# The first product of a feed-forward block in a two-layer decoder trunk: seven products instead of eight for three of eight row pairs

## The chip, the core and the metric

The kernel runs on one core of a Trainium2 chip, as one launch. The metric is device time in microseconds (us). Three runs of the kernel before gave 2171.43, 2171.99 and 2173.27 us; the median is 2171.99.

The engines are named as in the profile: PE (the matrix engine; PEld are its weight loads), DVE (vector), ACT (scalar), POOL, and SP, whose queue issues most DMAs. Every engine, and every queue, works through its instructions in the order in which they stand.

## The reference

256 tokens (T) of width 2048 (D) pass two layers. Each layer is a norm, a token mixer and a residual addition, then a norm, a SwiGLU feed-forward and a residual addition. The first mixer is a chunkwise mLSTM, the second a gated linear recurrence. All is float32. The part that changes is the feed-forward:

```python
D_FF = ((8 * D_MODEL // 3 + 255) // 256) * 256      # 5632

def swiglu(x, w_in, w_out):
    g, u = jnp.split(x @ w_in, 2, axis=-1)
    return (jax.nn.silu(g) * u) @ w_out

h = h + swiglu(rms_norm(h, norm_ffn[layer]), ffn_w_in[layer], ffn_w_out[layer])
```

x @ w_in is the first product (2048 rows of weights, 2 x 5632 columns), the one with w_out the second.

## The kernel before

**Precision.** A float32 product is made of three products in the type fp32r: every operand is split into hi (a cast, on ACT) and lo (operand minus hi, on DVE), and hi*hi, hi*lo and lo*hi are summed in one of eight PSUM banks. For weights, `halves` (L153) makes whi on ACT (L156) and wlo on DVE (L158) from the loaded tile raw; for features, `split_store` (L316) does it (L318, L319).

**Streaming.** `stream` (L165) goes through a weight matrix two rows of 128 (k, k + 1) and 512 columns at a time. Such a load is 512 KB on SP's queue (L77). The tiles raw, whi and wlo have four buffers each, so the fifth remainder wlo waits until PE has used up the first, and a load waits for the remainder made from its buffer. A scheduler orders the instructions of each engine when the program is built; weight preparation has a raised priority there.

**Two forms of product.** `linear_tok` (L179) has tokens on PSUM's partitions: the features are the stationary operand, the weights move, 512 columns a matmul (L187, L188, L189), six matmuls a row k for two blocks of 128 tokens. `linear_wide` (L208) has output features on the partitions: whi is stationary and hi and lo of the features (2 x 256 tokens) move together (L214), then wlo with hi (L217); eight matmuls a row k, four of 512 and four of 256 columns. `gather` (L223) then adds the two halves.

**The feed-forward** (`ffn`, L548) loops over eleven groups of 512 inner features. For each it makes g and u with `linear_wide` over 16 rows, gathers them, multiplies them by the norm's factor per token (a row spread over the partitions, `bc`), applies SiLU, multiplies, and splits the result into hh and hl (L319). After all eleven, `project_out` (L303) makes the second product with `linear_tok`: four output quarters (po) over 44 rows of inner features, each added to the residual h by DVE (L312).

**The norms.** `Norm.quarter` (L249) transposes a quarter of h (eight transposes, tr), scales it and splits it; it is queued in `pending` and run between two rows of the product that follows (`run_pending`, L148). `finish` (L288) makes the factor per token, and with `bcast` spreads it with a matmul (bc).

Of the kernel before, what the change touches and what calls it, by code (L numbers as in the profile page):

```python
# [27 lines left out]
AHEAD = 1000  # L28

# [4 lines left out]
def kernel(  # L34
# [111 lines left out]
    pending = []  # L146

    def run_pending():  # L148
        if pending:
            pending.pop(0)()  # L150
# [28 lines left out]
    def linear_tok(w, c0, nk, act, name, ncols=NB, lag=0):  # L179
# [12 lines left out]
        for k, hi, lo in stream(w, c0, nk, ncols):  # L192
# [4 lines left out]
            if k > 1:  # L197
                run_pending()
# [9 lines left out]
    def linear_wide(w, c0, nk, act, act2, name, soon=2):  # L208

        ps = [acc(f"{name}_{f}") for f in range(4)]  # L210
        for k, hi, lo in stream(w, c0, nk):
# [7 lines left out]
            if k >= soon:  # L219
                run_pending()  # L220
# [81 lines left out]

    def project_out(w, nk, act, nxt):  # L303

        for q in range(4):
            ps = linear_tok(w, q * NB, nk, act, f"po{q}", lag=nxt.lag if q == 3 else 0)
            for b in range(NT):
                if q == 3 and nxt.lag:
# [4 lines left out]
            if q < 3 or not nxt.lag:  # L313
                pending.append(lambda q=q: nxt.done(q))
# [34 lines left out]
    for q in range(1, 4):  # L349
        pending += [lambda q=q: n0.quarter(q), lambda: None]  # L350
    n1 = Norm("f0", par["g_ffn"][:, 0:16], bcast=True)

    def mlstm_mixer():
        with tc.tile_pool(name="mx", bufs=2) as mx:
            w = m_w_in[0]
            ys = [[mx.tile([P, 4, T], F32R, tag=f"y{s}{j}", name=f"y{s}{j}", bufs=1) for s in "hl"] for j in range(4)]
            sel = mx.tile([H, H, P], F32R, name="sel", bufs=1)
# [72 lines left out]
            pending.append(gate_rows)  # L430


            qT = mx.tile([P, H, T], F32, name="qT", bufs=1)
# [3 lines left out]
            def weights_of(hd):  # L437
# [17 lines left out]
                pr = mx.tile([P, 3 * P], F32, name=f"pr{hd}", tag="pr", bufs=8)  # L455
# [3 lines left out]
            for half in range(2):  # L459
# [9 lines left out]
                if half == 0:  # L469
                    pending.append(gate_cols)  # L470
                for hd in range(4 * half, 4 * half + 4):
                    pending.append(lambda hd=hd: weights_of(hd))
# [46 lines left out]
            for j in range(4):  # L519
# [8 lines left out]
                hn = mx.tile([P, NT, 2, DV], F32, tag="hn", name=f"hn{j}")  # L528
                for a in range(2):
                    pending.append(lambda a=a, j=j, vs=vs, hn=hn: head_out(j, a, vs, hn))  # L530
                ps = linear_tok(w, 4096 + j * NB, NK, n0.act, f"o{j}")
                y = mx.tile([P, NT, NB], F32, tag="y", name=f"y{j}", bufs=1)
# [8 lines left out]
                for i in range(2):  # L541
                    pending.append(lambda i=i, y=y, hi=hi, lo=lo, j=j: turn_y(j, i, y, hi, lo))
# [5 lines left out]
    def ffn(layer, n, nxt):  # L548
        with tc.tile_pool(name=f"ff{layer}", bufs=2) as fp:
            w = ffn_w_in[layer]  # L550
            hh, hl = [], []
            for j in range(FF // NB):
                pg = linear_wide(w, j * NB, NK, n.act, n.act2, f"g{j}")
                sg = fp.tile([P, 4, T], F32, tag="sg", name=f"sg{j}", bufs=1)
                gather(pg, sg)
# [213 lines left out]
```

## Time and profile before

| | |
|---|---|
| median of three runs | 2171.99 us |
| the profiled execution's own time | 2171.18 us |
| its span (first to last instruction) | 2169.4 us |
| mean granted clock of PE | 0.998 |
| PE, DVE, ACT busy, share of the span | 99%, 59%, 49% |
| first product of layer 0, from its first matmul | 396.94 to 888.71 us |

The span is 1.8 us shorter than the execution's own time. A line of a group reads: source line, engine, operation, output<-inputs, size, count | busy us, mean ns of one | idle time of the engine ahead of them, and what ended it. A line of the timeline reads: start, duration, engine, line, operation, with [idle time <- what ended it] behind it. A line of the windows reads: stretch, length, then PE, PEld, DVE, ACT and POOL busy (instructions), granted PE clock, DMA share, GB/s. Matmuls are pipelined: the next begins before the one ahead ends.

### The profile page before, as it was taken

How to read it: one execution, taken by the hardware profiler on the slowest of the kernel's cores; microseconds unless marked ns; L12 is line 12 of the kernel's file. 1: busy time of each engine (PE TensorE's matmuls, PEld its weight loads, DVE VectorE, ACT ScalarE, POOL GpSimd, SP SyncE). 2: the span in 40 equal slices, each digit the busy share in tenths (PEclk: the TensorE clock that was granted, in tenths of full speed). 3: DMA queues.
4: the chain of work that ended last, by engine and by line, in shares of the span. 5: the costliest groups of instructions: out<-in, count | busy, mean ns of one | idle time of the engine just before them, and what ended most of it. 6: DMA issues, size and time to landing. Idle time of an engine off the chain costs nothing.

```text
span 2169.4 us, 28888 instructions
## 1 busy us (share of the span) xinstructions
PE 2155.3 (99%) x11336; PEld 1841.6 (85%) x11336; DVE 1286.4 (59%) x1494; ACT 1067.9 (49%) x1389; POOL 44.1 (2%) x62
## 2 busy tenths in 40 slices
PE   9999999999999999999999999999999999999998
PEld 8888888888888888888888888888888888888886
DVE  6655555556565665554546797655656566554444
ACT  5445445544444444444446759554444444444433
POOL 0011110000000000000000000000000000000000
PEclk9999999999999999999999999999999999999999
DMA  7556655666666666555566665566666666665554
GB/s 224 169 165 180 180 178 190 182 188 189 189 187 192 187 192 186 192 191 188 194 191 184 181 186 183 184 183 188 191 187 192 187 191 188 190 209 194 194 184 155
DMA packets 211376, 405.82 MB, mean 187 GB/s; under 512 B 14552, under 2 KB 14760, under 8 KB 211112
## 3 DMA queue, kind: packets, MB, share of 16 engines
q1 hardware_dynamic: 210520, 401.89, 60.2%
q10 hardware_dynamic: 720, 2.10, 0.3%
q8 instruction: 88, 1.44, 0.3%
q14 instruction: 48, 0.39, 0.0%
HBM read 401.84 MB, written 2.10 MB: 186 GB/s over the span
## 4 chain that ended last, share of the span: by engine, by line
PE 96%; ACT 1%; DVE 1%; DMA 1%; issue 1%; POOL 0%; POOLq 0%; SPq 0%; ACTq 0%; DVEq 0%
PE u L214 15%; PE g L214 15%; PE po L188 10%; PE po L189 10%; PE po L187 10%; PE g L217 7%; PE u L217 7%; PE rec L214 3%; PE gb L214 2%; PE qk L214 2%; PE rec L217 1%; PE v L187 1%; PE v L189 1%; PE o L187 1%; PE v L188 1%; PE o L189 1%
## 5 line engine op out<-in xcount | busy, mean ns | idle before, releaser
L158 DVE TENSOR_TENSOR wlo<-raw,whi 128x1024 fp32r<-128x1024 f32 (+1 forms) x753 | 921.6, 1224 | 815.1 <-ACT whi L156 813.8
L156 ACT CAST whi<-raw 128x1024 fp32r<-128x1024 f32 (+1 forms) x753 | 791.5, 1051 | 949.0 <-PE po L189 350.5
L214 PE MATMUL g<-x_f,whi 128*128 128x512 f32 x1408 | 442.5, 396 | 0.0
L214 PE MATMUL u<-x_f,whi 128*128 128x512 f32 x1408 | 442.2, 395 | 0.0
L217 PEld LDWEIGHTS g<-x_f,wlo 128*128 128x128 f32 x1408 | 264.5, 188 | 62.5
L217 PEld LDWEIGHTS u<-x_f,wlo 128*128 128x128 f32 x1408 | 264.5, 188 | 62.5
L217 PE MATMUL g<-x_f,wlo 128*128 128x256 f32 x1408 | 276.6, 278 | 0.0
L217 PE MATMUL u<-x_f,wlo 128*128 128x256 f32 x1408 | 276.6, 278 | 0.0
L187 PE MATMUL po<-whi,hh 128*128 128x512 f32 x704 | 274.1, 389 | 0.0
L189 PE MATMUL po<-whi,hl 128*128 128x512 f32 x704 | 273.9, 389 | 0.0
L188 PE MATMUL po<-wlo,hh 128*128 128x512 f32 x704 | 273.9, 389 | 0.0
L214 PEld LDWEIGHTS g<-x_f,whi 128*128 128x128 f32 x1408 | 214.6, 189 | 0.3
L214 PEld LDWEIGHTS u<-x_f,whi 128*128 128x128 f32 x1408 | 214.3, 189 | 0.0
L188 PEld LDWEIGHTS po<-wlo,hh 128*128 128x128 f32 x704 | 132.2, 188 | 27.4
L189 PEld LDWEIGHTS po<-whi,hl 128*128 128x128 f32 x704 | 132.2, 188 | 27.4
L187 PEld LDWEIGHTS po<-whi,hh 128*128 128x128 f32 x704 | 132.2, 188 | 27.2
L214 PE MATMUL qk<-x_m,whi 128*128 128x512 f32 x256 | 81.1, 398 | 0.0
L214 PE MATMUL gb<-x_m,whi 128*128 128x512 f32 x256 | 80.7, 396 | 0.0
L214 PE MATMUL rec<-x_m,whi 128*128 128x512 f32 x256 | 80.6, 396 | 0.0
L217 PEld LDWEIGHTS rec<-x_m,wlo 128*128 128x128 f32 x256 | 48.1, 188 | 11.4
L217 PEld LDWEIGHTS gb<-x_m,wlo 128*128 128x128 f32 x256 | 48.1, 188 | 11.2
L217 PEld LDWEIGHTS qk<-x_m,wlo 128*128 128x128 f32 x256 | 47.9, 188 | 11.4 <-DVE wlo L158 0.2
(227 smaller groups left out, 2108.3 us busy)
## 6 DMA issues: line engine op xcount, KB each, us to landing
raw<-in_ffn_w_in_dram SPq DMA_DIRECT2D x352, 512.0 KB, 4.4
raw<-in_ffn_w_out_dram SPq DMA_DIRECT2D x176, 512.0 KB, 3.5
raw<-in_m_w_in_dram SPq DMA_DIRECT2D x95, 512.0 KB, 3.7
raw<-in_r_w_in_dram SPq DMA_DIRECT2D x64, 512.0 KB, 3.7
raw<-in_m_w_out_dram SPq DMA_DIRECT2D x32, 512.0 KB, 3.6
raw<-in_r_w_out_dram SPq DMA_DIRECT2D x32, 512.0 KB, 3.6
gr<-in_r_gate_w_dram SPq DMA_DIRECT2D x8, 512.0 KB, 3.2
h<-in_x_dram SPq DMA_DIRECT2D x4, 512.0 KB, 7.8
```

Source lines behind the costliest of these rows:

```text
L156: cast = nc.scalar.copy(hi[:, at, 0:ncols], r)
L158: nc.vector.tensor_tensor(lo[:, at, 0:ncols], r, hi[:, at, 0:ncols].bitcast(F32), op=ALU.subtract)
L187: nc.tensor.matmul(o, lhsT=ah[:, bs], rhs=hi, start=(k == 0), stop=False)
L188: nc.tensor.matmul(o, lhsT=ah[:, bs], rhs=lo, start=False, stop=False)
L189: nc.tensor.matmul(o, lhsT=al[:, bs], rhs=hi, start=False, stop=(k == nk - 1))
L214: nc.tensor.matmul(ps[f], lhsT=hi[:, f * P:(f + 1) * P], rhs=act2(k), start=(k == 0), stop=False, skip_group_check=True)
L217: nc.tensor.matmul(ps[f][:, 0:T], lhsT=lo[:, f * P:(f + 1) * P], rhs=act(k)[0], start=False, stop=(k == nk - 1), skip_group_check=True)
```

## The change

**Row pairs as 2x2 blocks.** For a group of 512 inner features, two rows k, k + 1 of weights and the two column blocks g and u form a 2x2 block matrix; two token blocks and two rows of features form another. The plain product takes eight block products, Strassen's form (Winograd's variant) seven, with sums of blocks ahead and behind. The change uses it for row pairs 2, 4 and 6 of the eight (`SEVEN`); all others stay plain. Tokens are on the partitions for all of them, each block product is three matmuls of 512 columns (hi*hi, hi*lo, lo*hi), and seven PSUM banks p1 to p7 add up over the eight pairs: a plain pair adds into p2, p4, p5 and p3, a seven into all. p1, p6 and p7 end with pair 6, the others with pair 7.

**Sums of features.** `Pairs` takes the place of `Norm` ahead of the feed-forwards. Its `quarter` makes, of a pair, the two rows' blocks for both token blocks and their sums or differences: seven forms for a seven, six for a plain pair.

**Sums of weights.** `seven(p)` loads both rows of g and u into one tile r (two buffers), splits three of the four blocks into sh and sl, makes the four sums in r on DVE, and splits those into th and tl. sh, sl, th and tl have one buffer each.

**Behind a group.** e1 to e4 combine the banks (seven additions or subtractions on DVE, one copy on ACT), SiLU is applied with the norm's factor as its scale (it is per partition now, so `bcast` is gone), and two products give the hidden features, tokens on partitions. `turn` transposes them (eight transposes, tile th with a group and a number) and splits them into hh and hl. It is queued with a delay: pending work now has a due time in `work`, the us of matmuls recorded so far.

**Four parts.** The eleven groups go in parts of 3, 3, 3 and 2 (`CHUNKS`); behind each, `project_out` makes the second product over that part's 12 or 8 rows alone and adds it to h, so h is added to four times. The norm that follows is fed by the last part alone. Tiles of the mixers (pr, sel, y, hn, th, a2, hs, ge) move into pools shared with the feature forms.

```diff
+
+SEVEN = (2, 4, 6)
+CHUNKS = ((0, 3), (3, 6), (6, 9), (9, 11))
...
     pending = []
-
-    def run_pending():
-        if pending:
-            pending.pop(0)()
+    work = [0.0]
+
+    def later(fn, after=0.0):
+        pending.append((work[0] + after, fn))
+
+    def run_pending(us, ready=True):
+        work[0] += us
+        if ready and pending and work[0] >= pending[0][0]:
+            pending.pop(0)[1]()
 
...
+    S_SLOT = {"s1": 0, "s2": 1, "s3": 2, "s4": 3, "a12": 4, "a22": 5, "a11": 6}
+    D_SLOT = {"d2": 0, "d1": 1, "a12": 2, "a22": 3, "a11": 4, "a21": 5}
+    scratch = {}
+    class Pairs(Norm):
+        def quarter(self, q):
+            for j in range(2):
+                p = 2 * q + j
+                seven = p in SEVEN
+                n = 7 if seven else 6
+                pt = misc(f"tr_{self.name}{q}{j}").rearrange("p (f t) -> p f t", f=2)
+                for f in range(2):
+                    for b in range(NT):
+                        c = (2 * p + f) * P
+                        nc.tensor.transpose(pt[:, f, b * P:(b + 1) * P], h[:, b, c:c + P], ident)
+                z = xpool.tile([P, 2, n, P], F32R, tag=f"{'xe'[j]}{q}", name=f"z{p}_{self.name}")
+                t = scratch["get"]().rearrange("p (s t) -> p s t", t=P)
+                for f in range(2):
+                    at = n - (3 if seven else 4) + 2 * f
+                    nc.scalar.activation(
+                        t[:, at:at + 2, :].rearrange("p s t -> p (s t)"), pt[:, f, :], AF.Copy,
+                        scale=self.gain[:, 2 * p + f:2 * p + f + 1],
+                    )
+                if seven:
+                    for o, a, b, op in ((0, 7, 5, ALU.subtract), (2, 6, 7, ALU.subtract),
+                                        (1, 0, 6, ALU.subtract), (3, 4, 1, ALU.add)):
+                        nc.vector.tensor_tensor(t[:, o, :], t[:, a, :], t[:, b, :], op=op)
+                else:
+                    nc.vector.tensor_tensor(t[:, 0:2, :], t[:, 2:6:2, :], t[:, 3:6:2, :], op=ALU.subtract)
+                split_store(z[:, 0], z[:, 1], t[:, 0:n, :])
+                self.x.append(z)
+
+        def form(self, p, name):
+            i = (S_SLOT if p in SEVEN else D_SLOT)[name]
+            return self.x[p][:, 0, i, :], self.x[p][:, 1, i, :]
...
+            if nxt and (q < 3 or not nxt.lag):
+                later(lambda q=q: nxt.done(q))
...
-    n1 = Norm("f0", par["g_ffn"][:, 0:16], bcast=True)
+    n1 = Pairs("f0", par["g_ffn"][:, 0:16])
...
+        with tc.tile_pool(name=f"ff{layer}", bufs=1) as fp:
+            scratch["get"] = lambda: fp.tile([P, 4 * T], F32, tag="hh2", name="zt")
+            w, wo = ffn_w_in[layer], ffn_w_out[layer]
+            wv = w.rearrange("(k p) n -> p k n", p=P)
+            cols = lambda j: (j * NB, FF + j * NB)
+            made = []
+
+            def group(j, hi, lo):
+                bank, begun = {}, set()
+                last = {i: (max(SEVEN) if i in (1, 6, 7) else 7) for i in range(1, 8)}
+
+                def add(i, p, name, bh, bl, end=True):
+                    if i not in bank:
+                        bank[i] = acc(f"p{i}_{j}")
+                    ah, al = n.form(p, name)
+                    o = bank[i]
+                    nc.tensor.matmul(o, lhsT=ah, rhs=bh, start=i not in begun, stop=False)
+                    nc.tensor.matmul(o, lhsT=ah, rhs=bl, start=False, stop=False)
+                    nc.tensor.matmul(o, lhsT=al, rhs=bh, start=False, stop=end and p == last[i])
+                    begun.add(i)
+
+                def plain(p):
+                    hl = []
+                    for c in cols(j):
+                        raw = load_raw(w, c, NB, 2 * p)
+                        hl.append(half_tiles(p))
+                        with tc.high_priority(offset=AHEAD):
+                            halves(raw, *hl[-1], slice(0, 2), NB, n0.evac[0])
+                    (h1, l1), (h2, l2) = hl
+                    for i, one, two, bh, bl in ((2, "a12", "a11", h1, l1), (4, "a22", "a21", h1, l1),
+                                                (5, "a22", "a21", h2, l2), (3, "d2", "d1", h2, l2)):
+                        add(i, p, one, bh[:, 0, :], bl[:, 0, :], False)
+                        add(i, p, two, bh[:, 1, :], bl[:, 1, :])
+
+                def seven(p):
+                    r = fp.tile([P, 4, NB], F32, tag="r", name=f"r{p}", bufs=2)
+                    for i, c in enumerate(cols(j)):
+                        nc.sync.dma_start(r[:, 2 * i:2 * i + 2, :], wv[:, 2 * p:2 * p + 2, c:c + NB])
+                    sh = fp.tile([P, 3, NB], F32R, tag="sh", name=f"sh{p}")
+                    sl = fp.tile([P, 3, NB], F32R, tag="sl", name=f"sl{p}")
+                    th = fp.tile([P, 4, NB], F32R, tag="th", name=f"th{p}")
+                    tl = fp.tile([P, 4, NB], F32R, tag="tl", name=f"tl{p}")
+                    with tc.high_priority(offset=AHEAD):
+                        split_store(sh, sl, r[:, 0:3, :])
+                        nc.vector.tensor_tensor(
+                            r[:, 1:4:2, :], r[:, 1:3, :], r[:, 3:4, :].broadcast_to([P, 2, NB]), op=ALU.add
+                        )
+                        nc.vector.tensor_tensor(r[:, 2, :], r[:, 1, :], r[:, 2, :], op=ALU.add)
+                        nc.vector.tensor_tensor(r[:, 0, :], r[:, 2, :], r[:, 0, :], op=ALU.add)
+                        split_store(th, tl, r)
+                    for i, name, bh, bl, c in ((1, "a11", sh, sl, 1), (2, "a12", sh, sl, 0), (3, "s4", sh, sl, 2),
+                                               (5, "s1", th, tl, 1), (6, "s2", th, tl, 2), (7, "s3", th, tl, 3),
+                                               (4, "a22", th, tl, 0)):
+                        add(i, p, name, bh[:, c, :], bl[:, c, :])
+
+                def tmp(tag):
+                    return fp.tile([P, NB], F32, tag=tag, name=f"{tag}{j}")
+
+                for p in range(8):
+                    if p in SEVEN:
+                        seven(p)
+                    else:
+                        plain(p)
+                    run_pending(4.76 if p in SEVEN else 5.44)
+                    if p == max(SEVEN):
+                        e1, e2, e3 = tmp("e1"), tmp("e2"), tmp("e3")
+                        nc.scalar.copy(e1, bank[1])
+                        nc.vector.tensor_tensor(e2, bank[6], e1, op=ALU.add)
+                        nc.vector.tensor_tensor(e3, bank[7], e2, op=ALU.add)
+                e4 = tmp("e4")
+                nc.vector.tensor_tensor(e1, bank[2], e1, op=ALU.add)
+                nc.scalar.activation(e1, e1, AF.Silu, scale=n.rstd[:, 0:1])
+                nc.vector.tensor_tensor(e4, bank[4], e3, op=ALU.add)
+                nc.scalar.activation(e4, e4, AF.Silu, scale=n.rstd[:, 1:2])
+                nc.vector.tensor_tensor(e2, bank[5], e2, op=ALU.subtract)
+                nc.vector.tensor_tensor(e3, bank[5], e3, op=ALU.subtract)
+                nc.vector.tensor_tensor(e2, bank[3], e2, op=ALU.add)
+                for b, u, g in ((1, e3, e4), (0, e2, e1)):
+                    nc.vector.scalar_tensor_tensor(
+                        out=u, in0=u, scalar=n.rstd[:, b:b + 1], in1=g, op0=ALU.mult, op1=ALU.mult
+                    )
+
+                def turn(i):
+                    made.append((j, i))
+                    pt = misc(f"th{j}{i}").rearrange("p (f t) -> p f t", f=2)
+                    for f in range(2):
+                        for b, u in enumerate((e2, e3)):
+                            c = (2 * i + f) * P
+                            nc.tensor.transpose(pt[:, f, b * P:(b + 1) * P], u[:, c:c + P], ident)
+                    split_store(hi[:, 2 * i:2 * i + 2, :], lo[:, 2 * i:2 * i + 2, :], pt)
+
+                for i in range(2):
+                    later(lambda i=i: turn(i), 4.0 + i)
+
+            for c0, c1 in CHUNKS:
+                hid = []
+                for j in range(c0, c1):
+                    hi = fp.tile([P, 4, T], F32R, tag=f"hh{j - c0}", name=f"hh{j}")
+                    lo = fp.tile([P, 4, T], F32R, tag=f"hl{j - c0}", name=f"hl{j}")
+                    hid.append((hi, lo))
+                    group(j, hi, lo)
+                def hidden(k):
+                    while (c0 + k // 4, k % 4 // 2) not in made:
+                        pending.pop(0)[1]()
+                    return tuple(t[:, k % 4, :] for t in hid[k // 4])
+
+                project_out(wo[c0 * NB:c1 * NB, :], 4 * (c1 - c0), hidden, nxt if c1 == FF // NB else None)
```

The order of the instructions at three places follows. The first is DVE inside a group. Before, in group 10 of layer 0 (sg is g gathered), it makes remainders of weights and gathers now and then:

```order
L158 TENSOR_TENSOR wlo4_7490<-raw4_7487,whi4_7489 128x1024
L226 TENSOR_TENSOR sg10_7428<-g10_0_7248,sg10_7428 128x256
L226 TENSOR_TENSOR sg10_7428<-g10_1_7249,sg10_7428 128x256
L158 TENSOR_TENSOR wlo6_7512<-raw6_7509,whi6_7511 128x1024
L226 TENSOR_TENSOR sg10_7428<-g10_2_7250,sg10_7428 128x256
L226 TENSOR_TENSOR sg10_7428<-g10_3_7251,sg10_7428 128x256
L556 TENSOR_TENSOR sg10_7428<-sg10_7428,rbc_f0_3426 128x1024
```

Now, in group 4 of layer 0, between the seven of pair 4 (sl4, the three sums in r4, tl4) and that of pair 6 (sl6) stand the two remainders of plain pair 7 (wlo7):

```order
L363 TENSOR_TENSOR sl4_5302<-r4_5298,sh4_5301 128x1536
L645 TENSOR_TENSOR r4_5298<-r4_5298 128x2x512
L648 TENSOR_TENSOR r4_5298<-r4_5298 128x512
L649 TENSOR_TENSOR r4_5298<-r4_5298 128x512
L166 TENSOR_TENSOR wlo7_5413<-raw14_5410,whi7_5412 128x1024
L363 TENSOR_TENSOR tl4_5304<-r4_5298,th4_5303 128x2048
L166 TENSOR_TENSOR wlo7_5419<-raw14_5416,whi7_5418 128x1024
L363 TENSOR_TENSOR sl6_5373<-r6_5369,sh6_5372 128x1536
```

Five operations of a seven have come in, one behind the other, and the gathering is gone. The second place is DVE behind the last group ahead of a second product. Before, the last steps on group 10 (v10) and the first weights of the second product (wlo8, wlo10) alternate:

```order
L226 TENSOR_TENSOR v10_7619<-u10_3_7442,v10_7619 128x256
L561 TENSOR_TENSOR v10_7619<-v10_7619,rbc_f0_3426 128x1024
L158 TENSOR_TENSOR wlo8_7711<-raw8_7708,whi8_7710 128x1024
L562 TENSOR_TENSOR v10_7619<-v10_7619,sg10_7428 128x1024
L158 TENSOR_TENSOR wlo10_7729<-raw10_7726,whi10_7728 128x1024
L319 TENSOR_TENSOR hl10_7631<-v10_7619,hh10_7630 128x1024
```

Now, behind group 2 of layer 0, the last group of the first part (e_ are its sums, tl2 belongs to group 3, wlo8 and wlo10 to the first output quarter, wlo0_4491 and wlo2_4509 to the second):

```order
L166 TENSOR_TENSOR wlo10_4469<-raw10_4466,whi10_4468 128x1024
L675 TENSOR_TENSOR e22_4309<-p5_2_4064,e22_4309 128x512
L363 TENSOR_TENSOR tl2_4906<-r2_4900,th2_4905 128x2048
L166 TENSOR_TENSOR wlo0_4491<-raw0_4488,whi0_4490 128x1024
L166 TENSOR_TENSOR wlo2_4509<-raw2_4506,whi2_4508 128x1024
L676 TENSOR_TENSOR e32_4310<-p5_2_4064,e32_4310 128x512
L677 TENSOR_TENSOR e22_4309<-p3_2_4071,e22_4309 128x512
L679 SCALAR_TENSOR_TENSOR e32_4310<-e32_4310,rstd_f0_3442,e42_4350 128x512
L679 SCALAR_TENSOR_TENSOR e22_4309<-e22_4309,rstd_f0_3442,e12_4308 128x512
L363 TENSOR_TENSOR hl2_4037<-th20_4392,hh2_4036 128x512
L363 TENSOR_TENSOR hl2_4037<-th21_4405,hh2_4036 128x512
```

The last four operations on the group now stand behind two remainders of the second output quarter. Layer 1 has the same order there. The third place is PE at the same point. Before, in the second product, eight rows of inner features in (hh1 and hl1 end, hh2 begins), it goes straight on:

```order
L187 MATMUL po0_1_7635<-whi6_7692,hh1_4156 128x512
L188 MATMUL po0_1_7635<-wlo6_7693,hh1_4156 128x512
L189 MATMUL po0_1_7635<-whi6_7692,hl1_4157 128x512
L187 MATMUL po0_0_7634<-whi8_7710,hh2_4542 128x512
L188 MATMUL po0_0_7634<-wlo8_7711,hh2_4542 128x512
L189 MATMUL po0_0_7634<-whi8_7710,hl2_4543 128x512
```

Now the transposes of group 2 (th20, th21, of e22 and e32) stand between the same two steps:

```order
L196 MATMUL po0_1_4361<-wlo6_4433,hh1_3712 128x512
L197 MATMUL po0_1_4361<-whi6_4432,hl1_3713 128x512
L689 MATMUL th20_4392<-ident_74,e22_4309 128x128
L689 MATMUL th20_4392<-ident_74,e32_4310 128x128
L689 MATMUL th20_4392<-ident_74,e22_4309 128x128
L689 MATMUL th20_4392<-ident_74,e32_4310 128x128
L689 MATMUL th21_4405<-ident_74,e22_4309 128x128
L689 MATMUL th21_4405<-ident_74,e32_4310 128x128
L689 MATMUL th21_4405<-ident_74,e22_4309 128x128
L689 MATMUL th21_4405<-ident_74,e32_4310 128x128
L195 MATMUL po0_0_4360<-whi8_4450,hh2_4036 128x512
L196 MATMUL po0_0_4360<-wlo8_4451,hh2_4036 128x512
```

What PE does next there needs those transposes, and they need the two L679 above. On PE the program has 9,693 rows now, 11,125 before.

More of the change, by code (lines that the diff above doesn't have):

```diff
@@ L196, in linear_tok @@
                 block(1, *late.pop(0))
[L197 to L198 removed]
+            run_pending(1.36, k > 1)
         for kt in late:
@@ L349 @@
     for q in range(1, 4):
-        pending += [lambda q=q: n0.quarter(q), lambda: None]
-    n1 = Norm("f0", par["g_ffn"][:, 0:16], bcast=True)
+        later(lambda q=q: n0.quarter(q))
+        later(lambda: None)
+    n1 = Pairs("f0", par["g_ffn"][:, 0:16])
     def mlstm_mixer():
```

64 lines of the change are left out of this document (23 added, 41 removed).

## The prediction

> **What bounds the kernel now.** I read the page first, then the timeline of the matrix engine, the groups by line and form, and the busy times by stage. The page gives the frame: the span, each engine's share, and the chain that ended last.
>
> ```profile
> span 2169.4 us, 28888 instructions
> PE 2155.3 (99%) x11336; PEld 1841.6 (85%) x11336; DVE 1286.4 (59%) x1494; ACT 1067.9 (49%) x1389; POOL 44.1 (2%) x62
> PE 96%; ACT 1%; DVE 1%; DMA 1%; issue 1%; POOL 0%; POOLq 0%; SPq 0%; ACTq 0%; DVEq 0%
> PEclk9999999999999999999999999999999999999999
> ```
>
> The chain is PE almost from end to end, at full clock. The feed-forward stages say the same: first product of layer 0, then its second product, with PE never idle and DVE at 60% and 50%.
>
> ```profile
> 398.00:889.00 491.00, 491.00 (x2824) 428.52 (x2823) 295.02 (x311) 234.55 (x294) 0.73 (x1) 1.00 0.64 189
> 889.00:1131.00 242.00, 242.00 (x1081) 200.66 (x1080) 121.12 (x113) 102.74 (x116) 0.00 (x0) 1.00 0.57 191
> ```
>
> So a PE instruction less is worth its spacing, as long as DVE and ACT keep up. A busy time is no spacing, because matmuls overlap; I take the spacing from starts. The first product of layer 0 runs from its first matmul to the first of the second product:
>
> ```profile
> 396.94 0.62 PE L214 MATMUL g<-x_f,whi 128*128 128x512 f32 x2
> 888.71 0.40 PE L187 MATMUL po<-whi,hh 128*128 128x512 f32 x1
> ```
>
> That is 491.8 us for 11 groups, 44.7 each (the eight transposes of the last quarter and the broadcast matmul are in it).
>
> **The change, part by part.**
>
> *Fewer matmuls.* The new first product issues only 128x512 matmuls with their own weights each, in the manner of the second product. Two rows of the second product, 60 matmuls apart, give their spacing, and two rows around eight transposes give theirs:
>
> ```profile
> 1336.80 0.39 PE L189 MATMUL po<-whi,zl 128*128 128x512 f32 x1
> 1350.40 0.39 PE L189 MATMUL po<-whi,zl 128*128 128x512 f32 x1
> ...
> 1134.97 1.03 PE L258 MATMUL tr_m<-ident,h 128*128 128x128 f32 x8
> 1135.84 0.60 PE L299 MATMUL bc_m<-dg_m,ones 128*128 128x256 f32 x2
> ```
>
> 13.60 / 60 = 0.2267 us a matmul, 0.87 us for eight transposes. A plain pair has 24 matmuls (5.44 us), a pair of seven products 21 (4.76), a group 5 x 24 + 3 x 21 = 183, or 41.5 us. Turning the hidden features to the partition side adds eight transposes a group, 0.87, so 42.35. A layer: 11 x 42.35 plus the last quarter's 0.87 = 466.8 against 491.8, or 25.0 less. **Two layers: -50.0 us.** PE's work can give no more than that.
>
> *Does DVE keep up?* The rows that price DVE and ACT work (mean ns of one):
>
> ```profile
> L158 DVE TENSOR_TENSOR wlo<-raw,whi 128x1024 fp32r<-128x1024 f32 x751 | 920.3, 1226 | 815.1 <-ACT whi L156 813.8
> L312 DVE TENSOR_TENSOR h<-po,h 128x512 f32<-128x512 f32 x30 | 19.2, 683 | 0.0
> L156 ACT CAST whi<-raw 128x1024 fp32r<-128x1024 f32 x751 | 790.4, 1053 | 949.0 <-PE po L189 350.5 <-PE g L214 230.4 <-PE u L214 216.3
> L244 ACT ACTIVATE junk<-h 128x512 f32<-128x512 f32 x38 | 24.0, 630 | 0.6
> L187 PE MATMUL po<-whi,hh 128*128 128x512 f32 x704 | 274.1, 389 | 0.0
> ```
>
> 1536 and 2048 elements have no row; going on by the step from 512 to 1024 (0.54 us on DVE, 0.42 on ACT), DVE takes 1.77 and 2.31 us, ACT 1.48 and 1.90. In proportion to the 1024 row they would be 1.84 and 2.45 on DVE; I take the step, since the 512 and 1024 rows lie on it, and keep the other (0.6 us a group) for the range. A group then has on DVE ten weight remainders (12.26), three sevens of 1.77 + 1.23 + 2 x 0.68 + 2.31 = 6.67 (20.0), and seven sums, two products and two remainders of hidden features at 0.683 (7.5): 39.8 us of PE's 42.35. Started back to back they come a little closer, 1.14 us apart:
>
> ```profile
> 713.34 1.23 DVE L561 TENSOR_TENSOR v<-v,rbc_f 128x1024 f32<-128x1024 f32 x1
> 714.48 1.22 DVE L158 TENSOR_TENSOR wlo<-raw,whi 128x1024 fp32r<-128x1024 f32 x1
> 715.61 1.22 DVE L562 TENSOR_TENSOR v<-v,sg 128x1024 f32<-128x1024 f32 x1
> ```
>
> which makes 36.6 at best. So DVE goes from 60% to about 90%, and ACT (ten casts, three of 1.48 and of 1.90, five of 0.63) has 23.8 us. On average both fit; the order is what can fail.
>
> *Waits inside a group.* The tiles of a seven (sh, sl, th, tl) have one buffer. From the third product of one seven to the first use of tl in the next, PE has 12 + 24 + 9 + 3 matmuls, 10.9 us. In that time run the chain: matmul end (0.389 - 0.227 = 0.16 behind its spacing), cast of sh 1.48, sl 1.77, sums 1.23 + 0.68 + 0.68, cast of th 1.90, tl 2.31 = 10.2 us, and five hand-overs of 0.03 as between these:
>
> ```profile
> 701.97 1.05 ACT L156 CAST whi<-raw 128x1024 fp32r<-128x1024 f32 x1 [1.69 <-PE u L214]
> ...
> 703.05 1.22 DVE L158 TENSOR_TENSOR wlo<-raw,whi 128x1024 fp32r<-128x1024 f32 x1 [1.51 <-ACT whi L156]
> ```
>
> 10.4 of 10.9. But ACT casts the next plain pair's first half ahead of th, and that cast may start only when PE has left the plain pair's first half, so th starts 0.5 late: the slack is used up, some 0.1 us of waiting in each of two sevens. The transposes of the group before come after DVE's last product, also about 0.1 late: 0.3 us in a steady group (j = 4, 5, 7, 8, 10). The first three groups have another order, in which sl of pair 4 follows the transposes and the product behind them; DVE idles there for 0.87 + 0.68 + 0.2 and the cast's 1.48, so a round takes it 39.8 + 3.2 = 43.0 us: 0.7 in each of groups 1 and 2, and 0.5 in group 0, where DVE also makes the last quarter's forms. Groups 3, 6 and 9 start after DVE had room. That is 5 x 0.3 + 2 x 0.7 + 0.5 = 3.4 us a layer, **+6.8**; the low end is 0.
>
> *Waits at the end of a part.* The second product of a part of three groups needs the third group's hidden features after eight steps (48 matmuls, 10.9 us). In the first part, DVE's queue has two remainders of the second output quarter (wlo0, wlo2) ahead of the last four operations on that group. wlo2's buffer is freed by the very last of those eight steps. So PE stops there, and waits for: 0.16, cast of whi2 1.05, wlo2 1.23, four operations of 0.683 = 2.73, four transposes 0.44 + 0.16, cast of the hidden features 0.63, hand-overs 0.3: 6.7 us, of which 0.87 are the transposes counted already. **5.8 us, twice: +11.6.** Queued behind wlo2 on DVE are those four operations alone; PE waits for them and ACT for PE. In the second and third parts only wlo0 stands ahead of the last product, so the transposes come some 0.9 late and hl 0.3 more: 1.2 each, **+4.8** for four. In the last part nothing stands ahead.
>
> *The clock.* Such a wait can cost more than itself. In the trace PE waited 0.20 and 1.31 us, and then 8 matmuls ran 0.43 apart at half clock, 3.4 us long:
>
> ```profile
> 1352.35 0.73 PE L187 MATMUL po<-whi,zh 128*128 128x512 f32 x2 [0.20 <-ACT whi L156]
> 1354.39 0.50 PE L188 MATMUL po<-wlo,zh 128*128 128x512 f32 x1 [1.31 <-DVE wlo L158]
> 1355.42 0.61 PE L187 MATMUL po<-whi,zh 128*128 128x512 f32 x1
> 1358.82 0.40 PE L189 MATMUL po<-whi,zl 128*128 128x512 f32 x1
> ```
>
> ```profile
> 1356.00:1358.00 2.00, 2.00 (x7) 1.52 (x6) 2.00 (x4) 0.00 (x0) 0.00 (x0) 0.50 0.65 226
> 1228.00:1230.00 2.00, 0.44 (x3) 0.44 (x4) 2.00 (x3) 1.88 (x4) 0.00 (x0) 1.00 0.88 326
> ```
>
> That is 3.4 - 8 x 0.227 = 1.6 us; another wait, in the second window, left the clock at 1.00. I count 1.6 for both long waits and for half of the four short ones: **+6.4**. The low end is 0. [...]
>
> *What costs nothing.* The second product in four parts has as many matmuls; its 24 more additions to h a layer (0.683 each, 16.4 us) lie on DVE beside the 242 us of PE in the second row above, where DVE is 50% busy; without that cover they would cost 16.4. Gathering, the broadcast multiply and the two 1024-wide products fall away on DVE and ACT, which were not waited for. Weights: as many bytes, in loads of the same size; a pair of seven is asked for when tl two pairs earlier is made, some 9 us before its cast, and this row says 4.4 to landing:
>
> ```profile
> raw<-in_ffn_w_in_dram SPq DMA_DIRECT2D x352, 512.0 KB, 4.4
> ```
>
> SP's queue is in order, so a load for a seven that waits for its buffer holds the plain loads behind it, but in the same reckoning these have over 5 us too. The tiles that move to other pools in the mixers keep one owner at a time: 0, give or take 2.
>
> **Sum.** 2171.2 (the profiled execution's own time, 0.8 below the median of 2171.99) - 50.0 + 6.8 + 11.6 + 4.8 + 6.4 = 2150.8; on the scale of the median **2152 us**, or 20 less. A measurement of this kernel can tell about 0.2% (4.3 us) from no change.
>
> **Rivals.**
> 1. *PE alone bounds.* DVE packs its work closer (36.6 us), the short waits vanish and only the two long ones stay: 2172 - 50 + 11.6 = 2134. For it: the 1.14 us spacing. Against it: the chain through one buffer does not get shorter by packing.
> 2. *Part of the gain lost.* One seven in each group finds its chain 0.9 us late, by the dearer 1536 and 2048 (0.08 + 0.14) and one more cast ahead of th than I see: 22 x 0.9 = +20, 2172: no change.
> 3. *DVE and ACT become the bound, slower than before.* Place: the one-buffered sh to tl chain of pairs 4 and 6. If on chip one remainder of a plain pair (1.226) falls into that chain each time, with no slack left, it costs 2 x 1.226 x 22 = +54: 2206. It decides from 1.1 us of extra waiting a group on (0.55 a seven), for then 24 us are gone. For it: 10.4 of 10.9 us are needed, DVE is at 90%, and its queue is in order. Against it: the same durations held within 1% all over the trace of before.
>
> **Chances.** Forecast (2140 to 2165) 0.54; first rival 0.18; second (2165 to 2178) 0.14, of it 0.04 faster, 0.09 the same, 0.01 slower; third 0.14. Faster 0.54 + 0.18 + 0.04 = 0.76, same 0.09, slower 0.15. The range 2130 to 2178 leaves out the third rival and the low third of the first (0.06). The forecast's own range is 2140 to 2165: 6.8, 4.8 and 6.4 at nothing or nearly doubled.
>
> **What would show it.** Right: about 183 matmuls of 0.227 a group; steady groups of 42.5 to 43 us; DVE near 90% in the first product; PE idle for 5 to 6 us, released by DVE's last product, once at the first part's end in each layer; the clock at half behind it. Wrong: DVE never waiting and groups of 44 us or more (third rival); no idle stretch at the first part's end; PE waiting for a load.

## The result and the profile after

The changed kernel takes 2151.7 us (median of four runs, 2149.2 to 2155.8), the kernel before 2172.6 on the same chip. The ratio is 0.9906, 95% interval 0.9889 to 0.9923: faster by 0.9%. The profiled execution took 2150.69 us, 20.5 less than that of before.

The page of the changed kernel has the same frame, with fewer matmuls and a busier DVE, and with PE's share of the chain down from 96% to 92%:

```profile
span 2148.9 us, 26007 instructions
PE 2120.2 (99%) x9902; PEld 1757.5 (82%) x9902; DVE 1566.6 (73%) x1732; ACT 1121.7 (52%) x1293; POOL 44.1 (2%) x62
...
PE 92%; DVE 3%; ACT 2%; issue 1%; DMA 1%; SPq 0%; POOL 0%; POOLq 0%; ACTq 0%; DVEq 0%
...
L363 DVE TENSOR_TENSOR tl<-r,th 128x2048 fp32r<-128x2048 f32 x66 | 151.1, 2290 | 35.6 <-ACT th L362 35.6
L363 DVE TENSOR_TENSOR sl<-r,sh 128x1536 fp32r<-128x1536 f32 x66 | 115.9, 1757 | 23.4 <-ACT sh L362 23.2
```

The last two rows are the operations for which the kernel before had no row: 2.29 and 1.76 us, where the step from 512 to 1024 had given 2.31 and 1.77.

The windows of the changed kernel by stage: groups 0-2, their part of the second product, groups 3-5 (three steady groups), their part, then groups 0-2 of layer 1 and their part.

```profile
397.20:526.90 129.70, 128.76 (x575) 104.87 (x574) 111.62 (x110) 74.25 (x71) 0.73 (x1) 1.00 0.62 205
526.90:599.70 72.80, 67.84 (x297) 55.89 (x296) 44.24 (x46) 29.42 (x29) 0.00 (x0) 0.98 0.64 200
599.70:726.85 127.15, 127.15 (x566) 104.26 (x565) 108.02 (x101) 65.64 (x59) 0.00 (x0) 1.00 0.60 191
726.85:793.90 67.05, 66.66 (x297) 54.81 (x296) 40.64 (x41) 28.71 (x28) 0.00 (x0) 1.00 0.66 203
...
1418.40:1549.00 130.60, 128.83 (x575) 104.91 (x575) 111.67 (x110) 74.15 (x71) 0.69 (x1) 1.00 0.62 204
1549.00:1622.70 73.70, 68.74 (x297) 56.58 (x296) 44.22 (x46) 29.42 (x29) 0.00 (x0) 0.95 0.63 197
```

A steady group, one behind the first three of a layer, takes 127.15 / 3 = 42.4 us, and DVE is busy for 85% of it (36.0 us). The first part of the second product is 6 to 7 us longer than the next one, with as many matmuls. The timeline of DVE and then of PE shows why:

```profile
535.57 2.28 DVE L363 TENSOR_TENSOR tl<-r,th 128x2048 fp32r<-128x2048 f32 x1
537.77 2.54 DVE L166 TENSOR_TENSOR wlo<-raw,whi 128x1024 fp32r<-128x1024 f32 x2
540.23 0.68 DVE L676 TENSOR_TENSOR e<-p,e 128x512 f32<-128x512 f32 x1
540.83 0.68 DVE L677 TENSOR_TENSOR e<-p,e 128x512 f32<-128x512 f32 x1
541.43 1.40 DVE L679 SCALAR_TENSOR_TENSOR e<-e,rstd_f,e 128x512 f32<-128x512 f32 x2
```

```profile
537.54 0.39 PE L197 MATMUL po<-whi,hl 128*128 128x512 f32 x1
542.89 1.97 PE L689 MATMUL th<-ident,e 128*128 128x128 f32 x8 [4.96 <-DVE e L679]
544.68 0.79 PE L195 MATMUL po<-whi,hh 128*128 128x512 f32 x1
545.27 0.63 PE L196 MATMUL po<-wlo,hh 128*128 128x512 f32 x1
```

PE stops at 537.9 us and waits 4.96 us for the products of group 2 (L679), ahead of which DVE makes two weight remainders for the next output quarter. The eight transposes then take 1.79 us from start to start instead of 0.79, at half clock. Layer 1 has the same wait, 4.96 us.

### The profile page after: what moved, and what is told of

It is laid out like the page before. It is cut to its first block, busy times and chain, and to the rows that moved or that the text cites. A ratio compares the mean times of both kernels' runs of the same rounds, so it can differ in the third digit from the quotient of the medians.

```text
span 2148.9 us, 26007 instructions
## 1 busy us (share of the span) xinstructions
PE 2120.2 (99%) x9902; PEld 1757.5 (82%) x9902; DVE 1566.6 (73%) x1732; ACT 1121.7 (52%) x1293; POOL 44.1 (2%) x62
## 4 chain that ended last, share of the span: by engine, by line
PE 92%; DVE 3%; ACT 2%; issue 1%; DMA 1%; SPq 0%; POOL 0%; POOLq 0%; ACTq 0%; DVEq 0%
PE p L616 14%; PE p L615 14%; PE p L617 14%; PE po L195 9%; PE po L196 9%; PE po L197 9%; PE rec L221 3%; PE gb L221 2%; PE qk L221 2%; PE rec L224 1%; PE v L195 1%; PE v L196 1%; PE o L195 1%; PE v L197 1%; PE o L197 1%
## 5 line engine op out<-in xcount | busy, mean ns | idle before, releaser
L166 DVE TENSOR_TENSOR wlo<-raw,whi 128x1024 fp32r<-128x1024 f32 (+1 forms) x621 | 757.6, 1222 | 446.6 <-ACT whi L164 445.7
L164 ACT CAST whi<-raw 128x1024 fp32r<-128x1024 f32 (+1 forms) x621 | 652.3, 1052 | 800.4 <-PE po L197 326.3
L615 PE MATMUL p<-whi,z_f 128*128 128x512 f32 x880 | 342.8, 390 | 0.0
L616 PE MATMUL p<-wlo,z_f 128*128 128x512 f32 x880 | 342.6, 389 | 0.0
L617 PE MATMUL p<-whi,z_f 128*128 128x512 f32 x880 | 342.2, 389 | 0.0
L615 PEld LDWEIGHTS p<-whi,z_f 128*128 128x128 f32 x880 | 165.2, 188 | 34.6 <-DVE e L669 0.4
L617 PEld LDWEIGHTS p<-whi,z_f 128*128 128x128 f32 x880 | 165.2, 188 | 34.4
L616 PEld LDWEIGHTS p<-wlo,z_f 128*128 128x128 f32 x880 | 165.2, 188 | 34.2
L363 DVE TENSOR_TENSOR tl<-r,th 128x2048 fp32r<-128x2048 f32 x66 | 151.1, 2290 | 35.6 <-ACT th L362 35.6
L197 PEld LDWEIGHTS po<-whi,hl 128*128 128x128 f32 x704 | 132.5, 188 | 27.9 <-DVE hl L363 0.4
L362 ACT CAST th<-r 128x2048 fp32r<-128x2048 f32 x66 | 126.1, 1910 | 28.2 <-PE p L617 16.0
L363 DVE TENSOR_TENSOR sl<-r,sh 128x1536 fp32r<-128x1536 f32 x66 | 115.9, 1757 | 23.4 <-ACT sh L362 23.2
L617 PE MATMUL p<-th,z_f 128*128 128x512 f32 x264 | 103.3, 391 | 0.0
L615 PE MATMUL p<-th,z_f 128*128 128x512 f32 x264 | 86.1, 391 | 2.7 <-ACT th L362 2.7
```

The lines of the kernel that those rows point to most:

```text
L164: cast = nc.scalar.copy(hi[:, at, 0:ncols], r)
L166: nc.vector.tensor_tensor(lo[:, at, 0:ncols], r, hi[:, at, 0:ncols].bitcast(F32), op=ALU.subtract)
L197: nc.tensor.matmul(o, lhsT=al[:, bs], rhs=hi, start=False, stop=(k == nk - 1))
L362: nc.scalar.copy(dst_hi, src)
L363: nc.vector.tensor_tensor(dst_lo, src, dst_hi.bitcast(F32), op=ALU.subtract)
L615: nc.tensor.matmul(o, lhsT=ah, rhs=bh, start=i not in begun, stop=False)
```

## The experiments

Eight kernels tell the parts apart. All ratios are against the kernel before, which ran beside them on the same chip; its medians there were 2171.7 to 2172.5 us.

**The last operations of a part moved ahead on DVE.** The lines L670 to L679 stand in a block with raised priority where the group is the last of its part:

```diff
+                with tc.high_priority(offset=2 * AHEAD if j in [c[1] - 1 for c in CHUNKS] else 0):
+                    e4 = tmp("e4")
+                    nc.vector.tensor_tensor(e1, bank[2], e1, op=ALU.add)
...
```

> The changed kernel, with the last operations on the third group of each part (both activations and the additions and products behind them) given a higher priority, so that on DVE they stand ahead of the weight remainders of the second product's first two output quarters. Theory (the queue order on DVE makes the long waits, and the clock halves behind them): PE's waits of 4.96 us at the first part's end go, and with them the half clock behind; that stage comes from 72.8 and 73.7 us to about 67, as in the second and third parts, so 12 to 13 us less than the changed kernel: about 2139, ratio to the kernel before 0.985. Rival (the wait only moves: DVE is so full there that the remainders come late instead): a new wait of similar length on a weight remainder, 2148 to 2153.

Measured: 2135.2 us, ratio 0.9834 (0.9819 to 0.9848). DVE's timeline in that kernel, at the same place (the lines are one further on):

```profile
534.90 0.68 DVE L677 TENSOR_TENSOR e<-p,e 128x512 f32<-128x512 f32 x1
535.49 0.68 DVE L678 TENSOR_TENSOR e<-p,e 128x512 f32<-128x512 f32 x1
536.38 1.42 DVE L680 SCALAR_TENSOR_TENSOR e<-e,rstd_f,e 128x512 f32<-128x512 f32 x2 [0.20 <-ACT e L675]
537.71 2.35 DVE L166 TENSOR_TENSOR wlo<-raw,whi 128x1024 fp32r<-128x1024 f32 x2
```

Its windows: the first part in layer 0, the second part, the first part in layer 1.

```profile
527.20:593.90 66.70, 66.69 (x297) 54.71 (x296) 44.13 (x46) 29.21 (x29) 0.00 (x0) 1.00 0.68 221
...
721.00:787.30 66.30, 66.30 (x298) 54.88 (x298) 40.72 (x41) 28.70 (x28) 0.00 (x0) 1.00 0.67 206
1541.00:1607.80 66.80, 66.80 (x298) 54.75 (x298) 44.26 (x46) 29.22 (x29) 0.00 (x0) 1.00 0.68 222
```

The products are done at 537.8 instead of 542.8 us, the two remainders come behind them, and no new wait takes the place of the old one. The first parts are 6.1 and 6.9 us shorter, the four short waits of the later parts (0.8 each) are gone too: together some 16 of the 16.5 us. The theory had 12 to 13, since it left the short waits out. The queue order is shown as the cause, and this version beats both kernels.

**Two sevens in a group.** With the same priority, and `SEVEN = (2, 6)`.

> As the run with the higher priority for the last operations of a part, and pair 4 is a plain pair again: two pairs of seven in a group. Theory (PE's count of matmuls sets the time): three matmuls of 0.227 us more in each of 22 groups, +15.0 us, less up to 5 us since a seven no longer follows a seven two pairs behind, so that its tiles are free in time: 2149 to 2154. Rival (DVE, whose work falls by about 3.9 us a group, has been setting the pace): no slower than with three, 2140 or less.

Measured: 2140.3 us, 0.9854 (0.9838 to 0.9871): 5.1 more than with three, where the theory had 10 to 15 more and the rival nothing. Its window of groups 3-5:

```profile
593.20:721.90 128.70, 128.70 (x576) 106.25 (x575) 95.55 (x92) 62.81 (x60) 0.00 (x0) 1.00 0.57 188
```

Nine matmuls more would be 2.04 us; the stage is 1.6 us longer than its 127.1 with three. DVE is busy for 12.5 us less, and what three sevens lose there in waits for their tiles, 0.1 us each, is mostly gone. About half of what is missing from the 15 lies in the first three groups, 129.9 us with two and 129.8 with three: there the third seven is paid for in waits entirely. So the theory's sum holds with a larger return of waits, 10 us instead of 5; the rival's "no slower than with three" holds in the first three groups alone.

**Four sevens in a group.** With the same priority, and `SEVEN = (0, 2, 4, 6)`.

> As the run with the higher priority for the last operations of a part, and pair 0 is a pair of seven too: four in a group. Theory (PE's count of matmuls sets the time, with small waits for the tiles of a seven): -15.0 us against three, and up to +13 for 0.3 us at each of two more hand-overs in a group: 2124 to 2138. Rival (the chain through the one-buffered tiles and a DVE that is over 95% busy bound it): DVE's work in a group rises from 36.0 to about 39.9 us with PE's at 41.6, every hand-over comes 0.5 to 1 us late: 2145 or more.

Measured: 2153.7 us, 0.9917 (0.9902 to 0.9932), 18.5 more than with three. The total fits the rival, its reason only in small part. The steady groups of this kernel:

```profile
607.80:733.70 125.90, 125.89 (x558) 101.84 (x557) 116.82 (x107) 68.74 (x59) 0.00 (x0) 1.00 0.58 189
```

DVE is 93% busy, and three groups still take 1.2 us less than with three sevens (PE's count: 2.0 less). Most of the loss lies at the start of each layer. ACT's and SP's timelines, then PE's:

```profile
405.02 1.47 ACT L362 CAST sh<-r 128x1536 fp32r<-128x1536 f32 x1 [5.23 <-DMA r<-in_ffn_w_in_dram]
```

```profile
397.44 2.94 SPq L637 DMA_DIRECT2D r<-in_ffn_w_in_dram  x4
```

```profile
396.94 0.39 PE L197 MATMUL po<-whi,yl 128*128 128x512 f32 x1
406.54 1.65 PE L615 MATMUL p<-sh,z_f 128*128 128x512 f32 x3 [9.21 <-ACT sh L362]
```

The tile r lies in the feed-forward's own pool and its loads are issued when the mixer's last matmuls are done; a plain pair's weights come through a pool that is always there. So PE waits 9.2 us and starts at half clock, in both layers (9.4 us in layer 1). Groups 0-2 with their part lose another 4 to 5 us; about 2 of them are the half clock, and PE waits for sl or tl five times in those of layer 0, 0.3 to 0.4 us each, which is the rival's reason on a small scale. So a seven in pair 0 loses its gain at a layer's start, and not by a full DVE in the steady groups. That the late opening of the pool makes the loads late is read from these times; no run had r in another pool.

**The four parts alone.** The kernel before, with `project_out` called after groups 2, 5, 8 and 10 for their rows of `ffn_w_out`.

> The kernel before, with the inner features in four parts and nothing else: the first product stays with features on partitions, and the second product runs after groups 0-2, 3-5, 6-8 and 9-10, each part adding its sum to h. Theory: as many matmuls, and 24 more additions a layer hidden on DVE: 0 within 3 us of the kernel before, 2170 to 2176. Rival (the parts bring or cost something of their own, by waits at their ends or by weights that are loaded sooner): a difference of 5 us or more in either direction.

Measured: 2172.2 us, ratio 1.0000 (0.9990 to 1.0009). Nothing, as said. DVE rises by 28.9 us of busy time (1286.4 to 1315.3), all of it covered.

**No seven.** With the same priority, all pairs plain in the new layout, e1 to e4 reduced to two SiLUs, a copy, an addition and the two products.

```diff
-SEVEN = (2, 4, 6)
+SEVEN = ()
...
+                    nc.scalar.activation(e1, bank[2], AF.Silu, scale=n.rstd[:, 0:1])
+                    nc.scalar.activation(e4, bank[4], AF.Silu, scale=n.rstd[:, 1:2])
+                    nc.scalar.copy(e3, bank[5])
+                    nc.vector.tensor_tensor(e2, bank[3], e3, op=ALU.add)
```

> The changed layout without any pair of seven products: all eight row pairs plain, tokens on partitions, four parts, the last operations of a part at the higher priority. A group has 8 x 24 = 192 matmuls. Theory (PE's count and its spacing of 0.2267 us are all; the layout itself saves only what the count saves): a layer has 11 x 192 + 1056 matmuls, 718.2 us, eleven times eight transposes 7.9, and 3.6 for the quarters' transposes: 729.7 against 733.9 before, so 2164 and with small waits at the transposes as in the run with two sevens up to 2170. Rival (the layout, not the seven products, brings much of the gain): 2155 or less. Other rival (the layout costs and the seven products pay for it): over 2174.

Measured: 2169.3 us, 0.9990 (0.9981 to 1.0000), the upper end. PE never waits in its feed-forward; from the first matmul to the next mixer's:

```profile
397.25 0.39 PE L615 MATMUL p<-whi,z_f 128*128 128x512 f32 x1
...
1129.67 0.39 PE L221 MATMUL rec<-x_m,whi 128*128 128x512 f32 x1
```

732.4 us in layer 0, 1.4 less than before. A part of the second product takes 66.2 us there with one set of eight transposes, and 65.3 without in the run with the four parts alone: eight transposes cost 0.95 us between matmuls, not 0.87. So the layout by itself gives about 3 us in two layers, and the seven products bring the rest: 34 us lie between this run and the one with the last operations first.

**The chain of a seven ahead of plain weights.** With the same priority, and the block of sh, sl, sums, th and tl (L642) at `offset=AHEAD + 150`.

> As the run with the higher priority for the last operations of a part, and the operations on a seven's tiles (sh, sl, the sums, th, tl) stand some 150 places further ahead, so that fewer of the plain pairs' casts and remainders come between them on ACT and DVE. Theory (the small waits that are left, some 1.2 us in three steady groups and 2 us in the first three, come from plain casts ahead of th and remainders ahead of sl and tl): 3 to 8 us less, 2127 to 2132. Rival (the one buffer of each tile sets them: a chain of 10.4 us in 10.9 us whatever stands between): the same as without it, 2134 to 2137. Second rival (the plain pairs' weights come late instead): over 2138.

Measured: 2134.8 us, 0.9830 (0.9815 to 0.9845): nothing gained, as the rival had it, but the edit did not reach the place. ACT's timeline in a steady group of this kernel, at pair 6:

```profile
659.96 1.48 ACT L362 CAST sh<-r 128x1536 fp32r<-128x1536 f32 x1 [0.98 <-PE p L617]
665.53 1.05 ACT L164 CAST whi<-raw 128x1024 fp32r<-128x1024 f32 x1 [4.09 <-PE p L617]
666.49 1.91 ACT L362 CAST th<-r 128x2048 fp32r<-128x2048 f32 x1
```

The plain pair's first cast still stands ahead of th there, probably since the scheduler takes what is ready first; only pair 2's th moved. An order written by hand wasn't tried, so whether that cast's 0.5 us are the waits that are left stays open.

**Two buffers for sh, and its control.**

```diff
-                    sh = fp.tile([P, 3, NB], F32R, tag="sh", name=f"sh{p}")
+                    sh = fp.tile([P, 3, NB], F32R, tag="sh", name=f"sh{p}", bufs=2)
```

with raw at three buffers and rbc at one to make room; the control has raw at three alone.

> As the run with the higher priority for the last operations of a part, and the first tile of a seven's chain (sh) has two buffers instead of one, so that its cast needn't wait for the third product of the seven before; to make room, the weights' raw tile has three buffers instead of four, and the broadcast row of the norm one instead of two. The wait-free count for a layer's first and second product is 710.0 us (the run without sevens, 732.4, less 99 matmuls of 0.2267); the run with the priority alone takes 714.9. Theory (these 4.9 us come from the chain sh, sl, sums, th, tl that starts only when the one sh is free): most of it goes, 3 to 4 us a layer, 6 to 9 in all: 2126 to 2130. Rival (DVE's load as such makes them, whenever the chain may start): 2133 to 2137 as without. Second rival (the raw tile's third fewer buffers cost more): over 2138, and the run with that change alone shows it.

> The control of the run with two sh tiles: the higher priority for the last operations of a part, and three buffers for the weights' raw tile, sh with one. Theory (loads land within 4.5 us, and a step of the second product, which uses one such tile, takes 2.7 us): no change from the run with the priority alone, 2133 to 2138. Rival (the loads come late): 2140 or more, with PE's waits ending on a load or on the cast behind it.

Measured: 2157.1 us, 0.9927 (0.9913 to 0.9940), with two sh; the control 2138.5, 0.9847 (0.9833 to 0.9860), a little above the same kernel with four raw tiles, with intervals that overlap. So the second buffer made it 19 us slower. The second rival had a time over 2138, but not for its reason: the control has three raw buffers too and not the 19 us. The five runs with two sh lie between 2150.2 and 2157.9 us, and the trace is of the fastest. ACT's longest waits in it from 597 to 716 us, nearly all of groups 3-5 (us in total, times, longest):

```profile
ACT th L362 <- DVE r L649: 25.5, 5, 7.1
ACT whi L164 <- issue: 15.3, 3, 6.1
ACT whi L164 <- PE p L617: 7.9, 5, 1.7
ACT whi L164 <- DMA raw<-in_ffn_w_in_dram: 7.7, 3, 4.1
```

With sh free earlier the program was built in another order: the cast of th stands at the head of ACT's queue up to 7.1 us before DVE has made its sums, and the plain casts and with them the loads behind it are late. Whether the one sh buffer sets the 4.9 us a layer that are left stays open: the edit changed the order together with the buffer.

## Why the prediction was right

The time was 2152 predicted, 2151.7 measured, and the steps can be priced against the kernel without sevens. Its 732.4 us less 99 matmuls of 0.2267 is 710.0 us for a layer of the changed kernel without any wait, against 733.9 before. The changed kernel's layer 0:

```profile
397.18 0.39 PE L615 MATMUL p<-whi,z_f 128*128 128x512 f32 x1
...
1119.77 0.39 PE L221 MATMUL rec<-x_m,whi 128*128 128x512 f32 x1
```

722.6 us, so 12.6 of waits; layer 1, stage by stage in the same way, 14.3. In the table, the waits inside the groups are what is left of these 26.9 us when the other two kinds are taken off.

| term | predicted | measured |
|---|---|---|
| PE's work | -50.0 | -47.7 (2 x 23.9) |
| waits inside the groups | +6.8 | +9.4 |
| the two long waits and their half clock | +14.8 | +14.1 (6.6 and 7.5 above the wait-free part) |
| the four short waits and their half clock | +8.0 | +3.4 (4 x 0.85) |
| sum | -20.4 | -20.8; the two executions differ by 20.5 |

The terms are off by +2.3, +2.6, -0.7 and -4.6. That they cancel, and that the time came out within half a us, is luck; that the waits stand where they were put, all but one, is not.

- *Fewer matmuls.* Right but for the transposes, 0.95 us in the second product and 1.0 in the first (the kernel without sevens takes 132.5 us for groups 3-5, 576 matmuls are 130.6, and two sets stand in it) for 0.87: 22 x 0.1 is the difference.
- *DVE keeps up.* Right: 36.0 us a steady group, the low one of the two counts (36.6), so 85% and not 90%. 1536 and 2048 elements lay on the step.
- *Waits inside a group.* The chain held in its parts. In the kernel with the last operations first, a steady seven's sh cast starts at 659.98 us and tl ends at 670.72, 10.7 us; PE loses 0.1 us there, in two sevens a group, as said. What was too small is the first three groups: 2.4 and 3.2 us above the wait-free count, where 1.9 was said. A wait for th at the layer's start, 0.9 us in layer 0 and 1.8 in layer 1, was not in the reckoning; without it 1.5 and 1.4 are left. In layer 1, ACT and then PE:

```profile
1426.89 1.48 ACT L362 CAST sh<-r 128x1536 fp32r<-128x1536 f32 x1 [1.74 <-DMA r<-in_ffn_w_in_dram]
1436.03 1.20 PE L615 MATMUL p<-th,z_f 128*128 128x512 f32 x4 [1.77 <-ACT th L362]
```

  The chain of the first seven begins with a cast that waits for its load, and SP issues that load at 1418.73 us, 0.3 us behind the stage's first matmul. The prediction gave a seven's load some 9 us ahead of its cast and so put this at nothing; PE held up by a load was one of its signs of being wrong, and here it came at a small size. The run with four sevens has the same wait without two plain pairs ahead of it.
- *The long waits.* Right in place, in releaser and in the work ahead of it. Its chain up to the last product (0.16 + 1.05 + 1.23 + 2.73 = 5.2) took 4.96; the rest of the 5.8, the cast of the hidden features behind the transposes, was covered by the transposes of the other half.
- *The short waits.* The step that failed: the half clock. The end of the second part in the timeline, and the window behind it:

```profile
738.29 0.33 PE L689 MATMUL th<-ident,e 128*128 128x128 f32 x1 [0.39 <-DVE e L679]
```

```profile
738.00:742.00 4.00, 3.71 (x19) 3.00 (x20) 2.65 (x4) 2.05 (x3) 0.00 (x0) 1.00 0.97 333
```

  The wait is 0.39 us, 0.85 us with what goes with it where 1.2 was said, and the clock stays at 1.00, where 1.6 us were put down for each of two. Only the long ones were followed by half clock (0.50 from 542.4 and from 1563.0 us). With 1.6 us for these two alone the sum would have been 3.2 lower; the dearer waits in the first groups and the dearer transposes made up for that.
- *The rivals.* The first rival's 2134 lies near the 2135.2 of the run with the last operations first, but not by its reckoning: it kept the two long waits and dropped all others, and that run has lost the waits at the parts' ends and kept some 9 us inside the groups. The second, one seven of each group 0.9 us late, did not come: a steady group's sevens are 0.1 late. The third, a seven's chain that is late and DVE the bound, did not come at three sevens (85%), nor in the steady groups at four (93%).
- *The range.* With 6.8, 4.8 and 6.4 at nothing the sum is 2134 and not 2140, and with all three doubled 2170: the range given doesn't follow from them as it says.

## What to carry to other kernels

Count what an edit saves on the bound engine, then go through each engine's queue in its order at the places where one product ends and the next begins: here 17.5 of the 47.7 us saved went into waits at the ends of parts, and moving the last operations of a part ahead of the weight remainders gave 16.5 of them back. A loop that saves matmuls by vector work is worth extending only until its tiles come late, and by the traces its first use in a stage needs loads that are issued before the stage starts: with four sevens PE waited 9.2 and 9.4 us there. An extra buffer can change the order as well as the waiting (19 us lost here), so it has to be tried with its order looked at.

## What the hardware showed that was not expected

In the traces the half clock lasted 3.4 us, or two or three times as long. The changed kernel's windows around its two long waits, and those of the kernel with four sevens at its start:

```profile
537.90:542.40 4.50, 0.03 (x1) 0.00 (x0) 4.40 (x6) 1.04 (x1) 0.00 (x0) 1.00 0.78 244
542.40:545.80 3.40, 2.91 (x11) 2.46 (x12) 1.41 (x3) 1.17 (x2) 0.00 (x0) 0.50 0.89 312
545.80:546.50 0.70, 0.70 (x5) 0.56 (x4) 0.40 (x1) 0.00 (x0) 0.00 (x0) 1.00 0.12 47
1560.00:1563.00 3.00, 0.03 (x1) 0.00 (x0) 2.90 (x4) 1.04 (x1) 0.00 (x0) 0.99 0.68 203
1563.00:1569.80 6.80, 4.81 (x15) 3.98 (x16) 3.32 (x6) 1.17 (x2) 0.00 (x0) 0.50 0.65 235
```

```profile
397.40:400.50 3.10, 0.00 (x0) 0.00 (x0) 2.31 (x5) 2.36 (x5) 0.23 (x1) 1.00 0.77 251
400.50:410.70 10.20, 4.02 (x9) 2.72 (x10) 4.08 (x4) 1.47 (x1) 0.49 (x1) 0.50 0.63 237
410.70:412.00 1.30, 1.30 (x7) 1.08 (x6) 0.29 (x1) 0.89 (x1) 0.00 (x0) 0.99 0.00 0
```

3.4, 6.8 and 10.2 us: one, two and three stretches, beginning 4.5, 3.0 and 3.1 us after PE stopped. Two waits of the same 4.96 us so cost 6.6 and 7.5 us. The falls also keep a distance. The first four rows are those of the changed kernel, the other two those of the kernel before; the last row of each ends with the program, where PE has no more work:

```profile
542.39:545.80 3.41, 2.91 (x11) 2.46 (x12) 1.42 (x3) 1.17 (x2) 0.00 (x0) 0.50 0.89 312
1344.52:1347.93 3.41, 3.41 (x10) 2.64 (x9) 3.24 (x5) 0.86 (x2) 0.00 (x0) 0.50 0.62 187
1562.97:1569.80 6.83, 4.81 (x15) 3.98 (x16) 3.35 (x6) 1.17 (x2) 0.00 (x0) 0.50 0.66 236
2143.24:2148.89 5.65, 0.00 (x0) 0.00 (x0) 0.63 (x1) 1.21 (x2) 0.00 (x0) 0.50 0.54 211
```

```profile
1355.42:1358.83 3.41, 3.41 (x10) 2.63 (x9) 3.24 (x6) 0.81 (x2) 0.00 (x0) 0.50 0.65 201
2164.38:2169.39 5.01, 0.00 (x0) 0.00 (x0) 0.02 (x1) 0.60 (x1) 0.00 (x0) 0.50 0.53 209
```

From start to start these are 802.13, 218.45 and 580.27 us, and 808.96 in the kernel before. 802.13 / 235, 218.45 / 64, 580.27 / 170 and 808.96 / 237 are all 3.413 us: in each of these two executions the falls lie on one grid of that step.

On that grid one can look at the 3.41 us ahead of a fall. The first row is the kernel before, ahead of its half clock at 1355.4; the others are the changed kernel, ahead of the fall at 1563.0 and at the wait for th in layer 1, behind which the clock stayed at 1.00:

```profile
1352.01:1355.42 3.41, 1.91 (x7) 1.16 (x7) 3.41 (x4) 3.38 (x4) 0.00 (x0) 1.00 0.40 144
```

```profile
1559.56:1562.97 3.41, 0.47 (x3) 0.05 (x1) 3.31 (x5) 1.17 (x2) 0.00 (x0) 1.00 0.72 225
1433.26:1436.67 3.41, 1.64 (x8) 1.05 (x7) 3.07 (x6) 2.59 (x2) 0.00 (x0) 1.00 0.68 171
```

PE need not have been idle in them: the clock fell behind stretches in which it worked for 0.47 and for 1.91 us. But the clock did not fall behind one with 1.64 us, so PE's busy time in that stretch does not decide it alone, and no run here shows what does. The changed kernel has the half clock of the kernel before at the same place in the second mixer, 73.9 us ahead of the feed-forward, so it is no part of the difference.
